# Gate strips and modulation tiles in another order, and two rings for streamed tiles, in a hybrid mLSTM, retention and SSD layer

## The chip, the cores and the metric

The kernel runs on one core of a Trainium2 chip. The metric is the device time of one execution in microseconds, lower is better. The engines are named as the profile names them: PE multiplies matrices (PEld is its weight load), DVE, ACT and POOL work on vectors, SP issues the transfers between memory and the chip.

## What is computed

One layer of a trunk for 384 tokens of width 2048 (128 context tokens and 256 latent tokens, which share all weights). What matters of the reference:

```python
mod = silu(c) @ w_mod + b_mod
sh_a, sc_a, g_a, sh_f, sc_f, g_f = split(mod, 6)
h = rmsnorm(x, norm_mix_g) * (1 + sc_a) + sh_a
q, k, v, ..., gl = split(h @ w_in)
gates = sigmoid(gl)
merged = gates[0] * (y_m @ w_br_m) + gates[1] * (y_r @ w_br_r) + gates[2] * (y_s @ w_br_s)
x = x + g_a * (merged @ w_out)
h = rmsnorm(x, norm_mlp_g) * (1 + sc_f) + sh_f
x = x + g_f * (square(relu(h @ w_ff1)) @ w_ff2)
```

`y_m`, `y_r` and `y_s` are the outputs of three branches (mLSTM, retention, SSD), whose chunked scans also return final states. All is in float32.

## The kernel before

**Products.** Every large product is cut into strips, and a strip into units (`strip`, line 114). A unit streams 512 KB of weights: four blocks of 128 rows by 256 columns (kind A, 24 matmuls with 384 columns) or two blocks by 512 columns (kind B5, 18 matmuls with 512 columns). Each operand is split into a rounded high part and a rest, and three products are added. So for each unit ACT rounds the raw tile into `whi` (line 88, called in line 155), DVE subtracts it to get `wlo` (line 91, called in line 156), and then PE multiplies. There are 568 such units behind a start section of 32 units. Raw tiles have a ring of 6 buffers (`RAWB`, line 54), `whi` and `wlo` one of 3 (`SPB`).

**Order.** The order of the work is written out by the Python program: `run_units` (line 213) goes through the list of units. For each it emits the loads that the ring has room for (`emit_raws`, line 135, all on SP's queue), the split of the unit two ahead (`emit_splits`, line 143), the matmuls, one step of the generators in the background (`bg_steps`: the scans of the branches), up to `pops` entries of the modulation's queue (`pop_mods`, line 391), and the eviction of the strip that ended before. Each engine runs its instructions in the order in which they were emitted. `later(n, f)` emits f n units on.

**Modulation.** Four of the six modulation vectors are computed beside the products, in 16 quarters of 512 columns, and each quarter in 8 tiles of 512 KB of `w_mod`: 128 tiles. `strip` puts a tile behind a unit whenever a counter reaches 1 (lines 122 to 125); the counter grows by the stage's `rate` at each unit, and falls by 1 for a tile, by 3 for the last tile of a quarter. Before the change a tile takes its place in the ring of raw tiles, in the order of the list. `mod_tile` (line 334) then puts the tile's work into the queue: with `mx=2` four multiply-adds on DVE (line 339); with `mx=0` two of them on DVE, two scalings on ACT (line 348) and two additions on POOL. The raw buffer counts as free when that work has been emitted (`raw_done`, line 129), in the order of the ring. A quarter ends with matmuls that add its sums over the partitions (`mod_end`, line 356), behind two empty entries of the queue.

**Stages.** After the start section: mLSTM (strips for q, k, v of four heads and for the output gate, 64 units), the strips for the convolution (SX, 24 units), four gate strips of branch 0 and the strips for z (16 units each), retention in two halves of 24 units (RQ, RK, RV, line 1371) with three gate strips of branch 0 between them, retention's gate (RG, line 1380, 16 units), the merge (line 1455 on), `w_out` (32 units), and the two products of the MLP (4 times 32 units of `w_ff1` and 32 of `w_ff2`).

**Gates.** Gates of branch 1 are computed in the start section, and seven strips of branch 0 ahead by `gate_ahead` (line 1168): the sigmoid goes to DRAM (`scr_g`), and the merge loads it back (`g_load`, line 1391). The merge goes through `seq` (line 1389): branch 1, branch 0, branch 2, eight strips each of two units; a gate strip of four units stands ahead of a strip whose gate isn't there yet: one of branch 0, and all eight of branch 2, whose gate is also multiplied by `Rs` on POOL (line 1403). `b_evac` (line 1407) multiplies by the gate on DVE and adds to `mg` on POOL.

**End of the merge.** After the last gate strip `mh_begin` (line 1432) gives the room of the layer's input to `mhi` and `mlo` and splits 14 of the 16 blocks of `mg` (`mg_split`, line 1440: ACT rounds, DVE subtracts); `merged_end` splits the last two, and the `w_out` strips begin.

**Retention's scans.** `r_scan` (line 1238) is a generator with 12 steps for a pair of heads. The two pairs of the second half are put into the background when RV's second strip is evicted. The eviction of RG's strip p waits, by emitting steps with nothing between them, until pair p is done (`r_evac_g`, line 1351).

Of the kernel before, what the change touches and what calls it, by code (L numbers as in the profile page):

```python
# [11 lines left out]
ALU = mybir.AluOpType  # L12
# [3 lines left out]
D = 2048  # L16
# [30 lines left out]
def hybrid_step(ctx: ExitStack, tc: tile.TileContext, cpack, x_prompt, x_sample, c, state_mlstm_C,  # L47
# [6 lines left out]
    RAWB, SPB = 6, 3  # L54
# [52 lines left out]
    raw_list, unit_list = [], []  # L107
    raws, splits, done = {}, {}, set()
# [5 lines left out]
    def strip(w, c0, kt, operand, evac, kind="A", row0=0, post=None, pre=None, sync=False, hold=0):  # L114
# [3 lines left out]
        for k0 in range(0, kt, uk):  # L118
# [4 lines left out]
            if mods and tune["due"] >= 1:  # L123
                m = mods.popleft() + (tune["mx"],)
                tune["due"] -= 3 if m[2] == 7 else 1
                raw_list.append((mod_src(*m[:3]), 2))
                unit_list.append((Block("M", m, None, KT), len(raw_list) - 1, 0, 1))
# [14 lines left out]

    def emit_splits(n):
        while pos["split"] < min(n, len(unit_list)):
            i = pos["split"]
            blk, ri, k0, uk = unit_list[i]
            emit_raws()
            while ri not in raws:
                pop_mods(1)
                emit_raws()  # L150
            if blk.kind != "M":
# [61 lines left out]
    def run_units():  # L213
        for i, (blk, ri, k0, uk) in enumerate(unit_list):
# [7 lines left out]
            if blk.kind == "M":  # L222
                mod_tile(*blk.operand, raws.pop(ri), ri)
                continue
# [109 lines left out]
    def mod_tile(m, q, r, mx, t, ri):  # L334
        t = r3(t, 2)

        def first():
# [3 lines left out]
            if mx < 2:  # L341
                half.append(second)
            else:
                raw_done(ri)

        def second():
# [3 lines left out]
            raw_done(ri)  # L350

        dq.append(first)
        if r == 7:
            dq.extend((None, None, lambda: mod_end(m, q)))
# [569 lines left out]
    for h in range(4):  # L924
        tune.update(rate=0.65 if h else 0.0, pops=2)
# [234 lines left out]
    tune["rate"] = 0.0  # L1160
# [7 lines left out]
    def gate_ahead(b, j, pool_, tag):  # L1168
        def f(ps):
            for i in range(2):  # L1170
# [4 lines left out]
                act.activation(out=sg, in_=ps[i][:, 0:T], func=AF.Sigmoid)  # L1175
                later(1, lambda i=i, sg=sg: sp.dma_start(out=scr_g[b * KT + 2 * j + i], in_=sg))
# [3 lines left out]
    tune.update(rate=0.25, pops=2, mx=2)  # L1180
# [189 lines left out]
    tune.update(rate=0.35, pops=2, mx=2)  # L1370
    for p in range(2):
# [3 lines left out]
        if p == 0:  # L1375
            tune["rate"] = 0.65
            for j in (5, 6, 7):
                gate_ahead(0, j, "hl", None)
            tune["rate"] = 0.35
# [27 lines left out]
    def b_evac(n):  # L1407
        def f(ps):
            b, j = seq[n]
            mg, sg = P["mg"], GG.pop(n)  # L1410
            for i in range(2):
# [3 lines left out]
                else:  # L1415
                    tt(dve, sg[:, i], ps[i][:, 0:T], sg[:, i], ALU.mult)
                    tt(pool, mg[:, k], mg[:, k], sg[:, i], ALU.add)
            g_load(n + 2)
# [13 lines left out]
    def mh_begin():  # L1432
# [4 lines left out]
        for k in range(14):  # L1437
            mg_split(k)
# [16 lines left out]
    tune.update(rate=0.65, pops=2, mx=0)  # L1455
    after = {7: lambda: load_branch(y_m), 15: lambda: load_branch(P["y_s"]), 23: lambda: bg.append(merged_end())}
    for n, (b, j) in enumerate(seq):
        if (b, j) not in ahead:
            strip(W, GL + b * D + 256 * j, KT, h_op, g_evac(n), post=mh_begin if n == 23 else None)
# [3 lines left out]
    tune.update(rate=0.5, pops=2)  # L1463
# [187 lines left out]
    for fc in range(4):  # L1651
        for j in range(8):
            tune.update(rate=0.8 if j else 0.0, pops=2 if j else 0)
# [92 lines left out]
```

## Time and profile before

| | us |
|---|---|
| three runs, median (lowest to highest) | 2813.42 (2808.92 to 2814.22) |
| the profiled execution's own time | 2814.81 |
| its span, first to last instruction | 2813.0 |

The page of the profile gives each engine's busy time over the span. The prediction goes by stages: the table of stretches gives the same busy times for a part of the span, the clock that TensorE was granted there (1.00 is 2.4 GHz, and 0.5 the lower level of 1.2 GHz) and the rate of transfers. The waits of an engine in a stretch name the instruction that ended its idle time: "PE gb L100 <- DVE wlo L91" is a matmul of a strip that waited for the rest part of its weights. PE's matmuls overlap and their ends are modelled, so its idle time is a little smaller than what a stop costs.

### The profile page before, as it was taken

How to read it: one execution, taken by the hardware profiler on the slowest of the kernel's cores; microseconds unless marked ns; L12 is line 12 of the kernel's file. 1: busy time of each engine (PE TensorE's matmuls, PEld its weight loads, DVE VectorE, ACT ScalarE, POOL GpSimd, SP SyncE). 2: the span in 40 equal slices, each digit the busy share in tenths (PEclk: the TensorE clock that was granted, in tenths of full speed). 3: DMA queues.
4: the chain of work that ended last, by engine and by line, in shares of the span. 5: the costliest groups of instructions: out<-in, count | busy, mean ns of one | idle time of the engine just before them, and what ended most of it. 6: DMA issues, size and time to landing. Idle time of an engine off the chain costs nothing. (4 is left out here: it accounts for less than half of the span.)

```text
span 2813.0 us, 38264 instructions
## 1 busy us (share of the span) xinstructions
PE 2736.7 (97%) x15109; PEld 2513.9 (89%) x15109; DVE 1558.1 (55%) x1883; ACT 1155.7 (41%) x1708; POOL 757.4 (27%) x588
## 2 busy tenths in 40 slices
PE   8999999999999999999999998999999999999998
PEld 7899988898998988989999877988899899889987
DVE  3666566645765465567876756773343334334434
ACT  5333444546643343544444445442233233323333
POOL 4200233512241111235766442441100100010012
PEclk9999999999999999999999998999999999999999
DMA  9955555545755555466666643564443344344442
GB/s 316 307 191 171 144 173 153 167 143 157 214 149 155 155 181 163 144 191 208 193 200 189 230 158 120 184 201 140 127 128 128 128 128 127 127 128 127 127 144 103
DMA packets 377835, 465.54 MB, mean 165 GB/s; under 512 B 20980, under 2 KB 277128, under 8 KB 376504
## 3 DMA queue, kind: packets, MB, share of 16 engines
q1 hardware_dynamic: 377656, 463.10, 53.4%
q8 instruction: 118, 1.93, 0.3%
q14 instruction: 61, 0.50, 0.1%
HBM read 449.47 MB, written 13.57 MB: 165 GB/s over the span
## 5 line engine op out<-in xcount | busy, mean ns | idle before, releaser
L91 DVE TENSOR_TENSOR wlo<-raw,whi 128x1024 fp32r<-128x1024 f32 x599 | 817.5, 1370 | 954.0 <-ACT whi L88 944.5
L88 ACT ACTIVATE whi<-raw 128x1024 fp32r<-128x1024 f32 x600 | 632.3, 1058 | 1002.9 <-PE gb L100 465.0
L100 PE MATMUL gb<-hhi,whi 128*128 128x384 f32 x1600 | 552.0, 345 | 9.4 <-ACT whi L88 4.2
L100 PE MATMUL gb<-hhi,wlo 128*128 128x384 f32 x1600 | 540.9, 338 | 11.6 <-DVE wlo L91 11.5
L100 PE MATMUL gb<-hlo,whi 128*128 128x384 f32 x1600 | 538.1, 336 | 0.4 <-DVE hlo L91 0.4
L91 POOL TENSOR_TENSOR macc<-macc,raw 128x512 f32<-128x512 f32 x194 | 326.2, 1682 | 351.2 <-issue 245.7
L100 PE MATMUL gb<-h2i,wlo 128*128 128x384 f32 x1024 | 345.0, 337 | 5.1 <-DVE wlo L91 5.1
L100 PE MATMUL gb<-h2l,whi 128*128 128x384 f32 x1024 | 345.3, 337 | 3.7 <-DVE h2l L1553 3.7
L100 PE MATMUL gb<-h2i,whi 128*128 128x384 f32 x1024 | 344.9, 337 | 2.5 <-ACT h2i L1549 1.6
L339 DVE SCALAR_TENSOR_TENSOR macc<-raw,cs,macc 128x512 f32<-128x512 f32 x318 | 324.9, 1030 | 6.6 <-DMA macc<-in_b_mod_dram 0.7
L100 PEld LDWEIGHTS gb<-hhi,whi 128*128 128x128 f32 x1600 | 303.1, 189 | 25.1 <-issue 8.8
L100 PEld LDWEIGHTS gb<-hhi,wlo 128*128 128x128 f32 x1600 | 302.5, 189 | 17.5 <-DVE wlo L91 17.3
L100 PEld LDWEIGHTS gb<-hlo,whi 128*128 128x128 f32 x1600 | 303.0, 189 | 1.7 <-DVE hlo L91 0.7
L91 POOL TENSOR_TENSOR x<-x,t 128x512 f32<-128x512 f32 x45 | 71.7, 1623 | 801.7 <-DVE t L91 801.7
L100 PEld LDWEIGHTS gb<-h2i,wlo 128*128 128x128 f32 x1024 | 193.9, 189 | 7.0 <-DVE wlo L91 7.0
L100 PEld LDWEIGHTS gb<-h2l,whi 128*128 128x128 f32 x1024 | 193.7, 189 | 6.3 <-DVE h2l L1553 6.1
L100 PE MATMUL gb<-whi,ahi 128*128 128x512 f32 x512 | 199.3, 389 | 0.0
L100 PE MATMUL gb<-whi,alo 128*128 128x512 f32 x512 | 199.2, 389 | 0.0
L100 PE MATMUL gb<-wlo,ahi 128*128 128x512 f32 x512 | 199.2, 389 | 0.0
L100 PEld LDWEIGHTS gb<-h2i,whi 128*128 128x128 f32 x1024 | 193.9, 189 | 4.8 <-ACT h2i L1549 1.8
L348 ACT ACTIVATE raw<-raw,cs 128x512 f32<-128x512 f32 x194 | 134.0, 717 | 69.7 <-DVE macc L339 62.5
L100 PE MATMUL gb<-yhi,whi 128*128 128x384 f32 x384 | 129.2, 336 | 1.1 <-ACT yhi L88 1.1
(415 smaller groups left out, 3923.3 us busy)
## 6 DMA issues: line engine op xcount, KB each, us to landing
raw<-in_w_in_dram SPq DMA_DIRECT2D x264, 512.0 KB
raw<-in_w_ff_dram SPq DMA_DIRECT2D x256, 512.0 KB
raw<-in_w_mod_dram SPq DMA_DIRECT2D x128, 512.0 KB
mraw<-in_w_mod_dram SPq DMA_DIRECT2D x32, 1024.0 KB
raw<-in_w_out_dram SPq DMA_DIRECT2D x32, 512.0 KB
raw<-in_w_br_r_dram SPq DMA_DIRECT2D x16, 512.0 KB
raw<-in_w_br_m_dram SPq DMA_DIRECT2D x16, 512.0 KB
raw<-in_w_br_s_dram SPq DMA_DIRECT2D x16, 512.0 KB
```

Source lines behind the costliest of these rows:

```text
L88: act.activation(out=out, in_=in_, func=AF.Copy, **kw)
L91: eng.tensor_tensor(out=out, in0=a, in1=b, op=op)
L100: pe.matmul(out, l, r, start=start, stop=stop)
L339: dve.scalar_tensor_tensor(out=macc[:, v], in0=t[:, kk], scalar=cs[:, 2 * r + kk, v:v + 1], in1=macc[:, v], op0=ALU.mult, op1=ALU.add)
L348: act.activation(out=t[:, kk], in_=t[:, kk], func=AF.Copy, scale=cs[:, 2 * r + kk, 1:2])
```

## The change

- Raw weight tiles get a ring of 4, and modulation tiles a ring of 2 of their own (`mr`). A modulation tile's load is emitted when the tile before it is reached (`emit_mod`); if the tile two before it has not been emitted yet, entries of the queue are emitted until it has.
- `mod_end` stands behind three empty entries.
- The rates change: 0.65 to 0.55 in mLSTM, 0 to 0.35 (`mx=2`) for SX, 0.25 to 0.2 for gates and z, 0.35 (0.65 in the gate strips) to 0.55 in retention, 0.65 to 0.45 in the merge, 0.5 to 0.25 in `w_out`, 0.8 to 0.6 in the MLP.
- Seven of the eight gate strips of branch 2 move from the merge to between retention's second half and RG, through `gate_ahead`; its eviction multiplies them by `Rs` on POOL. They use the buffers "sg" of retention's pool.
- `mh_begin` comes at strip 16 of the merge instead of 23, and `mg_split` is emitted for two blocks after each strip of branch 2 instead of 14 times at once.

```diff
--- before.py
+++ after.py
@@ -51,7 +51,7 @@
                 final_norm_g, y_prompt, y_sample, new_C, new_n, new_m, new_ret, new_ssd):
     nc = tc.nc
     act, dve, pool, pe, sp = nc.scalar, nc.vector, nc.gpsimd, nc.tensor, nc.sync
-    RAWB, SPB = 6, 3
+    RAWB, MRB, SPB = 4, 2, 3
 
     class Pool:
         def __init__(self, name, side="left", space=None):
@@ -104,8 +104,8 @@
         pe.transpose(out, in_, ident[0:n, 0:n])
 
 
-    raw_list, unit_list = [], []
-    raws, splits, done = {}, {}, set()
+    raw_list, mod_list, unit_list = [], [], []
+    raws, mraws, splits, done, mdone = {}, {}, {}, set(), set()
     pos = {"raw": 0, "split": 0, "used": 0}
     pend_evac, bg, delayed = [], deque(), []
     tune = {"bg": 1, "rate": 0.0, "due": 0.0, "pops": 3, "mx": 0}
@@ -123,8 +123,8 @@
             if mods and tune["due"] >= 1:
                 m = mods.popleft() + (tune["mx"],)
                 tune["due"] -= 3 if m[2] == 7 else 1
-                raw_list.append((mod_src(*m[:3]), 2))
-                unit_list.append((Block("M", m, None, KT), len(raw_list) - 1, 0, 1))
+                mod_list.append(mod_src(*m[:3]))
+                unit_list.append((Block("M", m, None, KT), len(mod_list) - 1, 0, 1))
 
     def raw_done(i):
         done.add(i)
@@ -140,15 +140,19 @@
             raws[pos["raw"]] = t
             pos["raw"] += 1
 
+    def emit_mod(j):
+        if j < len(mod_list):
+            while j >= MRB and j - MRB not in mdone:
+                pop_mods(1)
+            mraws[j] = strm([128, 1024], "mr", bufs=MRB)
+            sp.dma_start(out=r3(mraws[j], 2), in_=mod_list[j])
+
     def emit_splits(n):
         while pos["split"] < min(n, len(unit_list)):
             i = pos["split"]
             blk, ri, k0, uk = unit_list[i]
-            emit_raws()
-            while ri not in raws:
-                pop_mods(1)
+            if blk.kind != "M":
                 emit_raws()
-            if blk.kind != "M":
                 s = raws.pop(ri)
                 hi = strm([128, 1024], "whi", bufs=SPB, dt=F32R)
                 lo = strm([128, 1024], "wlo", bufs=SPB, dt=F32R)
@@ -211,6 +215,7 @@
                     mm(o, al[:, q], wh, False, k == n)
 
     def run_units():
+        emit_mod(0)
         for i, (blk, ri, k0, uk) in enumerate(unit_list):
             if k0 == 0 and blk.sync:
                 flush_evac()
@@ -220,7 +225,8 @@
             if k0 == 0 and blk.pre:
                 blk.pre()
             if blk.kind == "M":
-                mod_tile(*blk.operand, raws.pop(ri), ri)
+                mod_tile(*blk.operand, mraws.pop(ri), ri)
+                emit_mod(ri + 1)
                 continue
             wh, wl = splits.pop(i)
             end = k0 + uk == blk.kt
@@ -341,17 +347,17 @@
             if mx < 2:
                 half.append(second)
             else:
-                raw_done(ri)
+                mdone.add(ri)
 
         def second():
             for kk in range(mx, 2):
                 act.activation(out=t[:, kk], in_=t[:, kk], func=AF.Copy, scale=cs[:, 2 * r + kk, 1:2])
                 tt(pool, macc[:, 1], macc[:, 1], t[:, kk], ALU.add)
-            raw_done(ri)
+            mdone.add(ri)
 
         dq.append(first)
         if r == 7:
-            dq.extend((None, None, lambda: mod_end(m, q)))
+            dq.extend((None, None, None, lambda: mod_end(m, q)))
 
     def mod_end(m, q):
         p = bank()
@@ -922,7 +928,7 @@
     W = w_in[0]
     bg.append(gates())
     for h in range(4):
-        tune.update(rate=0.65 if h else 0.0, pops=2)
+        tune.update(rate=0.55 if h else 0.0, pops=2)
         strip(W, MQ + 256 * h, KT, h_op, m_evac_q(h))
         strip(W, MK + 256 * h, KT, h_op, m_evac_k(h))
         if h % 2 == 0:
@@ -1157,7 +1163,7 @@
         r_begin()
         yield
 
-    tune["rate"] = 0.0
+    tune.update(rate=0.35, mx=2)
     strip(W, SX + 1024, KT, h_op, s_conv(4))
     strip(W, SX + 1280, KT, h_op, s_conv(5))
     for j in range(4):
@@ -1173,11 +1179,13 @@
                 else:
                     sg = P[pool_]([128, T], "ga_", tag="ylo%d" % (4 + (2 * j + i) % 4))
                 act.activation(out=sg, in_=ps[i][:, 0:T], func=AF.Sigmoid)
+                if b == 2:
+                    tt(pool, sg, sg, P["Rs"], ALU.mult)
                 later(1, lambda i=i, sg=sg: sp.dma_start(out=scr_g[b * KT + 2 * j + i], in_=sg))
         ahead.add((b, j))
         strip(W, GL + b * D + 256 * j, KT, h_op, f)
 
-    tune.update(rate=0.25, pops=2, mx=2)
+    tune.update(rate=0.2, pops=2, mx=2)
     for j in range(4):
         gate_ahead(0, j, "s", "ac")
     for j in range(4):
@@ -1367,16 +1375,16 @@
         g_load(0)
         g_load(1)
 
-    tune.update(rate=0.35, pops=2, mx=2)
+    tune.update(rate=0.55, pops=2, mx=2)
     for p in range(2):
         strip(W, RQ + 512 * p, KT, h_op, r_evac_qk(p, "q"), "B5")
         strip(W, RK + 512 * p, KT, h_op, r_evac_qk(p, "k"), "B5")
         strip(W, RV + 512 * p, KT, h_op, r_evac_v(p), "B5")
         if p == 0:
-            tune["rate"] = 0.65
             for j in (5, 6, 7):
                 gate_ahead(0, j, "hl", None)
-            tune["rate"] = 0.35
+    for j in range(1, 8):
+        gate_ahead(2, j, "r", "sg")
     for p in range(4):
         strip(W, RG + 256 * p, KT, h_op, r_evac_g(p), post=r_end if p == 3 else None)
 
@@ -1415,6 +1423,8 @@
                 else:
                     tt(dve, sg[:, i], ps[i][:, 0:T], sg[:, i], ALU.mult)
                     tt(pool, mg[:, k], mg[:, k], sg[:, i], ALU.add)
+                if b == 2 and j < 7:
+                    later(1, lambda k=k: mg_split(k))
             g_load(n + 2)
         return f
 
@@ -1434,8 +1444,6 @@
         P["mh"] = Pool("mh", "left")
         P["mhi"] = P["mh"]([128, KT, T], "mhi", dt=F32R)
         P["mlo"] = P["mh"]([128, KT, T], "mlo", dt=F32R)
-        for k in range(14):
-            mg_split(k)
 
     def mg_split(k):
         rnd(P["mhi"][:, k], P["mg"][:, k])
@@ -1452,15 +1460,15 @@
         x2_begin()
         yield
 
-    tune.update(rate=0.65, pops=2, mx=0)
+    tune.update(rate=0.45, pops=2, mx=0)
     after = {7: lambda: load_branch(y_m), 15: lambda: load_branch(P["y_s"]), 23: lambda: bg.append(merged_end())}
     for n, (b, j) in enumerate(seq):
         if (b, j) not in ahead:
-            strip(W, GL + b * D + 256 * j, KT, h_op, g_evac(n), post=mh_begin if n == 23 else None)
+            strip(W, GL + b * D + 256 * j, KT, h_op, g_evac(n), post=mh_begin if n == 16 else None)
         strip((w_br_m, w_br_r, w_br_s)[b][0], 256 * j, 8, y_op, b_evac(n), post=after.get(n))
 
 
-    tune.update(rate=0.5, pops=2)
+    tune.update(rate=0.25, pops=2)
     def x2_begin():
         P["x"] = Pool("px", "right")
         x2 = P["x2"] = P["x"]([128, 3, D], "x2")
@@ -1650,7 +1658,7 @@
 
     for fc in range(4):
         for j in range(8):
-            tune.update(rate=0.8 if j else 0.0, pops=2 if j else 0)
+            tune.update(rate=0.6 if j else 0.0, pops=2 if j else 0)
             strip(w_ff1[0], 2048 * fc + 256 * j, KT, h2_op, f1_evac(j), sync=fc == 0 and j == 0,
                   post=h2_end if fc == 3 and j == 7 else None)
         for n in range(4):
```

## Rows read from the trace of the kernel before

**Rows 1.** The page, part 1: the span, and PE's busy time with its share.

```profile
span 2813.0 us, 38264 instructions
PE 2736.7 (97%) x15109; PEld 2513.9 (89%) x15109; DVE 1558.1 (55%) x1883; ACT 1155.7 (41%) x1708; POOL 757.4 (27%) x588
```

**Rows 2.** Busy time by stretch: start:end, length, engines' us (count), PE clock, DMA, GB/s.

```profile
290.00:568.00 278.00, 264.73 (x1398) 244.79 (x1397) 173.28 (x269) 133.14 (x217) 108.81 (x77) 0.98 0.54 159
...
850.00:1120.00 270.00, 267.37 (x1334) 231.57 (x1333) 152.76 (x193) 99.93 (x145) 51.51 (x65) 1.00 0.55 164
1120.00:1222.00 102.00, 95.43 (x591) 93.42 (x590) 52.66 (x70) 52.19 (x96) 27.93 (x33) 0.98 0.44 131
1222.00:1568.00 346.00, 345.55 (x2020) 344.91 (x2019) 262.30 (x234) 158.07 (x207) 216.77 (x134) 1.00 0.65 201
1568.00:1715.00 147.00, 139.47 (x628) 113.00 (x627) 87.80 (x83) 67.22 (x109) 62.85 (x38) 1.00 0.58 198
...
1745.00:1880.00 135.00, 128.91 (x727) 124.19 (x726) 109.25 (x107) 68.91 (x101) 59.85 (x34) 1.00 0.61 185
1880.00:2740.00 860.00, 860.00 (x4334) 779.53 (x4333) 337.48 (x351) 270.02 (x320) 73.47 (x46) 1.00 0.42 132
```

**Rows 3.** PE's waits from 290 to 568 us (mLSTM): us in total, times, longest.

```profile
PE gb L100 <- DVE wlo L91: 8.8, 8, 1.8
PE gb L100 <- ACT whi L88: 4.3, 3, 2.1
```

**Rows 4.** SP's waits, whole span: weight loads behind POOL's modulation additions.

```profile
SPq L139 <- POOL macc L91: 302.1, 91, 8.9
```

**Rows 5.** ACT's waits, whole span: the largest on a weight load.

```profile
ACT whi L88 <- DMA raw<-in_w_out_dram: 12.1, 3, 5.8
```

**Rows 6.** PE's waits from 1180 to 1225 us (from RG to the merge).

```profile
PE sb L104 <- POOL o L91: 3.3, 1, 3.3
PE gb L100 <- ACT yhi L88: 1.1, 1, 1.1
PE sb L100 <- ACT kT L1281: 0.7, 1, 0.7
```

**Rows 7.** PE's waits from 1570 to 1595 us (first units of w_out).

```profile
PE gb L100 <- DVE wlo L91: 4.8, 3, 3.1
```

**Rows 8.** DVE in order of time, 1566 to 1577 us: start, us, instruction.

```profile
1565.52 9.46 DVE L91 TENSOR_TENSOR mlo<-mg,mhi 128x384 fp32r<-128x384 f32 x14 [0.94 <-ACT mhi L88]
1574.91 1.21 DVE L91 TENSOR_TENSOR wlo<-raw,whi 128x1024 fp32r<-128x1024 f32 x1
```

**Rows 9.** PE's waits from 1745 to 1880 us (first product of the MLP).

```profile
PE gb L100 <- DVE wlo L91: 5.1, 5, 1.2
```

**Rows 10.** PE's waits from 1595 to 1690 us (w_out).

```profile
PE gb L100 <- DVE wlo L91: 1.6, 2, 1.0
PE sb L100 <- POOL macc L91: 1.1, 1, 1.1
```

**Rows 11.** PE's waits from 860 to 1180 us (retention).

```profile
PE gb L100 <- DVE wlo L91: 1.0, 2, 0.8
```

**Rows 12.** DVE's groups from 850 to 1120 us (retention): busy us, mean ns.

```profile
L91 DVE TENSOR_TENSOR wlo<-raw,whi 128x1024 fp32r<-128x1024 f32 x59 | 72.9, 1248 | 81.6 <-ACT whi L88 76.8 <-PE sb L100 4.7
L339 DVE SCALAR_TENSOR_TENSOR macc<-raw,cs,macc 128x512 f32<-128x512 f32 x76 | 59.0, 797 | 1.3
L91 DVE TENSOR_TENSOR rt<-sb,cr 128x256 f32<-128x256 f32 x16 | 6.0, 420 | 8.0 <-POOL qtok L91 4.0 <-POOL ktok L91 4.0
```

**Rows 13.** DVE's and POOL's groups from 1222 to 1568 us (merge).

```profile
L91 DVE TENSOR_TENSOR wlo<-raw,whi 128x1024 fp32r<-128x1024 f32 x80 | 129.5, 1624 | 48.5 <-ACT whi L88 48.4
L339 DVE SCALAR_TENSOR_TENSOR macc<-raw,cs,macc 128x512 f32<-128x512 f32 x84 | 99.7, 1186 | 2.4 <-DMA macc<-in_b_mod_dram 0.7
...
L91 POOL TENSOR_TENSOR sg<-sg,Rs 128x384 f32<-128x384 f32 x15 | 21.2, 1435 | 3.3 <-ACT sg L1402 3.3
```

**Rows 14.** ACT in order of time, 1578 to 1585 us.

```profile
1583.69 0.53 ACT L88 ACTIVATE mhi<-mg 128x384 fp32r<-128x384 f32 x1 [4.41 <-POOL mg L91]
```

## The prediction

> **What bounds the kernel now.** The page comes first: PE is busy for 2736.7 of 2813.0 us [rows 1]. So the change, which leaves every product in place, can only win idle time of PE and time at the lower clock. The table of stretches tells where that is: PE idles 13.3 us in mLSTM (278 less 264.73), 2.6 in retention, 6.6 around RG, 0.5 in the merge, 7.5 in w_out, 6.1 in the first product of the MLP, and nothing in the 860 us from 1880 on, which have hardly any modulation tiles [rows 2]. The clock adds a little: 0.98 over 278 us costs 5.6 us, over the 102 us around RG 2.0.
>
> The waits say for what. In mLSTM 13.1 us are waits for `wlo` and `whi`, eleven stops of at most 2.1 us [rows 3]: no weights were missing, but ACT or DVE had other work ahead of the split. Around RG it is the scan of retention [rows 6], in w_out the split of `mg` [rows 7, 8] and tiles [rows 10], in the MLP tiles again [rows 9]. Loads are late less often: SP stood 302 us, 91 times, behind POOL's additions, because a raw buffer held a modulation tile [rows 4], yet the largest of five like groups in which ACT waited for a weight load is 12.1 us [rows 5].
>
> **The change part by part.** The sum is made against the profiled execution, 2814.81 us: the span and 1.8 us around it that stay. It stands 1.4 us above the median of the runs shown.
>
> Going through the counter of lines 122 to 125 with the old and the new rates gives where the 128 tiles fall, before and after: mLSTM 25 and 22, SX 0 and 6, the gates of branch 0 with z 7 and 5, retention with its three gate strips 19 and 27, the seven moved strips 0 and 12, RG 5 and 8, merge 44 and 19, w_out 10 and 5, first MLP product 18 and 14, the product behind it 0 and 10. Tiles with `mx=2` rise from 31 to 58: each swaps two scalings on ACT and two additions on POOL for two multiply-adds on DVE.
>
> 1. *End of retention.* The last two pairs of scans need 24 steps; between RV's end and the eviction of RG's last strip there are 16 units, one step each, so some eight steps run with nothing between them. That shows as PE waits of 3.3, 0.7 and, for what follows the late gate, 1.1 us, 5.1 of 6.6 us idle [rows 2, 6]; the clock fell in the same stretch. With the 28 units of the moved strips ahead of RG there are 44 units for 24 steps. I take 5 us and 1.5 of the clock's 2.0: **-6.5**, from -8 to -3 (the last split of `y_r` may still be late).
>
> 2. *Split of the merged blocks.* 14 subtractions run as one block of 9.46 us on DVE, with the next `wlo` behind them [rows 8]; PE waits 4.8 us at the first units of w_out [rows 7]. Two at a time behind each of seven strips, they lie beside 8 us of matmuls. **-4.5**, from -4.8 to -2.5 (the last two blocks stay at the end).
>
> 3. *mLSTM.* 13.3 us idle and 5.6 of clock over 25 tiles are 0.75 us for a tile. Three tiles fewer are 2.3; stops come where a tile meets scan work, so wider spacing helps more than in proportion. **-4**, from -9 (half of it) to +3 (the tiles fall on worse units).
>
> 4. *MLP.* 5.1 us of waits for `wlo` over 18 tiles [rows 9]. At a rate of 0.8 a unit has, on DVE, 0.8 x 2 multiply-adds of 1.19 us and a `wlo` of 1.62 (as in the merge, whose tiles are of the same kind [rows 13]), and evictions: close to a unit's 4.2 us (4,334 matmuls of rows 2 at 21 a unit, the mean of 24 and 18, are 206 units in 860 us). At 0.6 it is 0.5 us less, so runs of eight tiles no longer pile up; but ten tiles now fall into the second product. **-4**, from -6 to +3 (ten more at the same 0.3 us).
>
> 5. *w_out.* Ten tiles, 2.7 us [rows 10]; half of them. **-1**, from -2.7 to 0.
>
> 6. *SX.* Six tiles where none were. By retention's row, 1.0 us of waits over its tiles [rows 11], they cost 0.2 us; by mLSTM's 0.75 each, 4.5. They are of retention's kind (`mx=2`). **+1.5**, nearer to the first, as scans run here too.
>
> 7. *Tiles in retention.* 47 tiles where 24 were, over 104 units instead of 76. Each is four multiply-adds of 0.80 us on DVE [rows 12], 3.2 us at once. DVE was busy 57% here [rows 2]; 23 more tiles add 73 us, and 28 more units 35 of `wlo`, over 115 us more of PE. That makes some 65% to 70%, below the merge's 76%, where PE lost 0.5 us in 346 [rows 2]. Bounds by the row of retention, +1, and by mLSTM's 0.75 for each of 47 tiles, +34. I take **+3**: the work is bursty, but POOL is idle for 81% of the time.
>
> 8. *New waits.* `mg_split` on ACT now waits for POOL's addition with the next `whi` behind it; one such wait of 4.4 us is in the trace [rows 14] and cost PE under 0.2 us of rows 7, because splits run two units ahead. Seven of them: 0 to 1.4 us. The stores of the moved gates hold buffers that the scans' squares need, on DVE, ahead of `wlo`: four places, bounded by 0 and 1 us each. Fourteen stores and seven loads of 384 KB, and `mh_begin` at strip 16, are hidden under a rate of transfers that falls with the tiles. **+0.5**, from 0 to +5.
>
> 9. *The rings.* Weights now run four raw tiles ahead whatever POOL does, some 17 us at 4.2 us a unit. A full ring of six had 25, but only where no tile sat in it. What it can win is the part of ACT's waits [rows 5] that reached PE; against it, the modulation load waits on SP for the buffer of the tile two before, with weights behind it in the queue, up to 8.9 us [rows 4], which 17 us cover. A tile's load has two to four units ahead of its use. **-1**, from -3 to +2. The third empty entry of `mod_end` is nothing: one unit later, 16 times, beside other work.
>
> 10. *Gates and z.* Two tiles fewer: **-0.5**, from -1.5 to 0. The 25 tiles that leave the merge win nothing, as PE idles 0.5 us there.
>
> Sum: -6.5 - 4.5 - 4 - 4 - 1 + 1.5 + 3 + 0.5 - 1 - 0.5 = -16.5, so 2798.3 for an execution like the profiled one, and 1.4 less, **2797 us**, as a median.
>
> **A rule of the Trainium skill against one part.** In retention, with POOL busy 19% of the time, a `wlo` takes 1.25 us and a multiply-add 0.80; in the merge, with POOL at 63%, 1.62 and 1.19 [rows 2, 12, 13]. The Trainium skill (SBUF — State Buffer, section "SBUF: two separate sides") says that a DVE instruction with two SBUF inputs and a GpSimd (POOL) instruction that reads SBUF exclude each other for the whole instruction. By that rule the 14 multiplications by `Rs`, now on POOL amid retention's DVE work, each hold a DVE instruction for up to their own 1.44 us [rows 13], 20 us of DVE; were none of it hidden, the sum would be +3.5 and the time 2817. The rows speak for hidden: fifteen of them stood in the merge beside 0.5 us of idle PE [rows 2, 13].
>
> **The rivals.**
> *More is won.* If the stops of mLSTM come mostly from weights and splits that arrive late because tiles sit in their ring, all 18.9 us of term 3 could go instead of 4: 2782. For it: SP's 302 us [rows 4]. Against it: rows 3 name `wlo` and `whi`, and only a small part of ACT's waits are for loads [rows 5]. Chance 0.12.
> *The gain is given back.* Tiles cost the same wherever they stand: terms 3 to 5 vanish (+9), retention's 23 more tiles cost half of mLSTM's price (+8 instead of +3): 2797 + 9 + 5 = 2811. For it: the number of tiles is the same. Against it: the price of a tile in the rows goes from 0.04 to 0.75. Chance 0.14.
> *Slower.* DVE becomes the bound in bursts in retention. An eviction of RQ or RK has eight multiplications of 0.42 us (two groups of 16 like the one shown, over four evictions) [rows 12]: 3.4 us, two tiles 6.4, two `wlo` 2.5, together 12.3 us against the two units, 8.4 us, by which splits run ahead. If that happens at most evictions and in the scans too, a tile there costs what it costs in mLSTM, 0.75 us, 47 times: +34 instead of +3, 2828. It decides once retention's tiles cost over 0.4 us each. Against it: at the old rate it is 0.04. Chance 0.12.
> That the rings don't do what they say, because both kinds of load stay in one queue of SP, changes term 9 by 1 to 3 us and stays within the forecast.
>
> **How the numbers follow.** The forecast has 0.62, with a range of its own of 2786 to 2807 (terms 3, 4 and 7 some 10 us either way). The whole range, 2783 to 2815, reaches to the rival of a larger gain and takes in the gain given back; it leaves out the slower one and half of the larger gain. About 0.2% (5.6 us) is what a measurement can tell from no change: faster than 2807.8 is 0.73 (0.61 and 0.12), the same 0.15 (0.14 and 0.01), slower 0.12.
>
> **What would show it.** After: no wait of PE for `o` near RG's end and no low clock there; no block of 14 `mlo`; SP's waits on POOL's additions well below 302 us; PE idle in mLSTM about 10 us, in the MLP about 3, in retention under 8 over its longer stretch. The forecast is wrong if retention idles over 20 us, or if ACT or DVE wait long for loads of `mr`.

## The result, and the profile after

The changed kernel takes 2836.39 us (median of four runs, 2833.29 to 2839.46) beside 2812.18 (2808.92 to 2814.22) of the kernel before on the same chip: a ratio of 1.0083 [1.0070, 1.0095]. The forecast was 2797 us in a range of 2783 to 2815, so both the sign and the range were wrong.

PE's own line of the page shows 92.5 us in which it is not busy (2836.0 less 2743.5), where it was 76.3 before [rows 1]:

```profile
span 2836.0 us, 38143 instructions
PE 2743.5 (97%) x15109; PEld 2520.8 (89%) x15109; DVE 1521.5 (54%) x1937; ACT 1122.5 (40%) x1656; POOL 635.7 (22%) x534
```

The table of stretches answers to [rows 2], with the same columns. In order: start, mLSTM, retention, the moved gate strips, RG, merge, `w_out`, the first product of the MLP with its opening (norm and transposes), and this product behind its opening. The last line is the kernel before, for the same work as the line above it.

```profile
0.00:224.00 224.00, 200.59 (x1618) 177.78 (x1619) 118.23 (x217) 89.83 (x151) 48.58 (x48) 0.98 0.83 259
299.00:568.00 269.00, 260.02 (x1401) 243.00 (x1401) 165.30 (x263) 129.56 (x211) 98.42 (x71) 0.99 0.55 161
858.00:1143.00 285.00, 273.30 (x1341) 234.92 (x1340) 172.19 (x224) 98.42 (x143) 48.68 (x65) 0.98 0.54 166
1143.00:1293.00 150.00, 139.66 (x831) 136.49 (x830) 82.70 (x104) 62.58 (x105) 30.58 (x37) 0.98 0.54 163
1293.00:1362.00 69.00, 69.00 (x406) 69.00 (x405) 45.74 (x52) 24.46 (x31) 11.15 (x9) 1.00 0.63 200
1362.00:1602.00 240.00, 239.42 (x1398) 239.10 (x1397) 159.32 (x177) 99.81 (x131) 106.26 (x73) 1.00 0.62 200
1602.00:1736.00 134.00, 134.00 (x610) 110.09 (x609) 59.91 (x59) 55.75 (x90) 34.98 (x24) 1.00 0.54 187
1736.00:1893.00 157.00, 146.40 (x789) 140.18 (x789) 112.03 (x135) 83.00 (x138) 55.99 (x38) 0.93 0.50 154
1760.00:1893.00 133.00, 129.84 (x730) 127.41 (x731) 92.84 (x109) 68.94 (x103) 43.66 (x27) 0.99 0.56 170
...
1740.00:1880.00 140.00, 133.91 (x749) 129.19 (x749) 113.27 (x115) 72.60 (x109) 59.85 (x34) 0.99 0.59 179
```

What was aimed at was won: mLSTM idles 9.0 us where it was 13.3, RG and `w_out` not at all where they idled 6.6 and 7.5, and the first product of the MLP 3.2 behind its opening where it was 6.1. (The line from 1736 on, with 10.6 us and a clock of 0.93, has the opening in it, which [rows 2] leaves out: from 1738 to 1760 PE idles 7.5 of 22 us at a clock of 0.62, and in the kernel before, from 1717 to 1740, 7.6 of 23 at 0.68.) But retention idles 11.7 instead of 2.6 and the moved strips 10.3, and the start is 9 us longer. The waits of the whole span say what is late (the first two lines are SP's queue, the others PE, DVE and ACT):

```profile
SPq L139 <- DVE wlo L91: 1897.5, 524, 16.7
SPq L148 <- POOL macc L91: 80.9, 26, 7.5
...
PE gb L100 <- DVE wlo L91: 37.3, 30, 3.7
DVE macc L345 <- DMA macc<-in_b_mod_dram: 13.5, 5, 3.4
DVE W L837 <- DMA Tb<-scr: 11.2, 4, 3.2
PE gemv L100 <- DMA mraw<-in_w_mod_dram: 11.2, 7, 3.1
DVE macc L345 <- DMA mr<-in_w_mod_dram: 10.8, 8, 1.9
PE gb L100 <- ACT whi L88: 10.3, 7, 3.4
DVE jk L91 <- DMA scr_g<-ga__10169: 5.0, 1, 5.0
...
ACT whi L88 <- DMA raw<-in_w_in_dram: 3.3, 1, 3.3
```

Weights are no longer late: ACT's waits for weight loads are 3.3 us in all, where one of five groups alone had 12.1 [rows 5]. Late now are the transfers that stand between them on SP's queue: DVE waits 63 us for rows of `b_mod`, modulation tiles, the scans' inputs and stores of gates (the lines shown, the three other `jk` of 5.0, 4.9 and 4.9, `Cb` 4.5 and a state 3.1), where before it waited 9 us for transfers, of which `Cb` with 3.8 was the largest group. The timeline shows how one of them becomes late (start, duration, queue or engine; SP, then POOL, DVE and PE):

```profile
1937.38 0.38 SPq L139 DMA_DIRECT2D raw<-in_w_ff_dram  x1
1937.87 0.56 SPq L333 DMA_DIRECT2D macc<-in_b_mod_dram  x2
...
1932.82 0.95 POOL L338 MEMSET macc<- 128x1024 f32 x1 [14.89 <-DMA scr_mod<-macc]
...
1935.67 1.69 DVE L91 TENSOR_TENSOR wlo<-raw,whi 128x1024 fp32r<-128x1024 f32 x1
1940.75 4.00 DVE L345 SCALAR_TENSOR_TENSOR macc<-mr,cs,macc 128x512 f32<-128x512 f32 x4 [3.39 <-DMA macc<-in_b_mod_dram]
1944.67 4.51 DVE L91 TENSOR_TENSOR wlo<-raw,whi 128x1024 fp32r<-128x1024 f32 x2
...
1947.01 0.50 PE L100 MATMUL gb<-wlo,ahi 128*128 128x512 f32 x1 [2.46 <-DVE wlo L91]
```

POOL has cleared `macc` at 1933.77, and the row of `b_mod` could go there at once. But the weight load ahead of it on SP's queue goes into the buffer that DVE's subtraction frees, which ends at 1937.36. Only then do both transfers start. The row lands at 1940.7, DVE has stood 3.39 us for it, four multiply-adds follow, then two `wlo` that are late, and PE stops for 2.46 us.

This is not one case alone. From the end of POOL's clearing to the start of the row's transfer there are 0.0 us before (median of the 16 quarters) and 3.8 after. Of the 14 stores of moved gates, 12 start 2.1 to 2.6 us after POOL has finished the gate. The first of them stands behind a weight load that starts when a `wlo` ends, at 1175.23:

```profile
1172.16 1.02 POOL L91 TENSOR_TENSOR ga__10169<-ga__10169,Rs 128x384 f32<-128x384 f32 x1 [12.62 <-ACT ga__10169 L1181]
...
1173.44 1.79 DVE L91 TENSOR_TENSOR wlo<-raw,whi 128x1024 fp32r<-128x1024 f32 x1 [3.78 <-ACT whi L88]
...
1175.26 0.39 SPq L139 DMA_DIRECT2D raw<-in_w_in_dram  x1
1175.75 0.45 SPq L1184 DMA_DIRECT2D scr_g<-ga__10169  x1
```

From the first `whi` of a stage to the first of the next, the time went as follows (us against the kernel before, each from the one profiled execution; the last two columns are experiments told below):

| stage (term of the prediction) | forecast | after | one ring | three edits |
|---|---|---|---|---|
| start (none) | 0 | +9.1 | 0.0 | -1.6 |
| mLSTM (3) | -4 | -9.9 | -11.3 | -15.1 |
| SX (6) | +1.5 | +2.1 | +2.0 | +2.0 |
| gates of branch 0 and z (10) | -0.5 | +9.1 | +8.8 | +4.0 |
| retention with its gate strips (7) | +3 | +15.8 | +14.3 | +13.2 |
| moved strips, RG, merge (1) | -6.5 | -2.0 | -14.5 | -14.4 |
| `w_out` (2 and 5) | -5.5 | -3.6 | -3.7 | -3.7 |
| first two products of the MLP (4) | -4 | +2.4 | -8.4 | -5.7 |
| rest | 0 | 0.0 | 0.0 | 0.0 |
| sum (with terms 8 and 9, -0.5) | -16.5 | +23.0 | -12.8 | -21.3 |

In the MLP it is the second product that lost: 139.9 us from first `whi` to first `whi` instead of 130.0, the first one took 155.4 instead of 163.0 (by PE's own first matmuls 6.9 more and 4.5 less). The stop of the timeline stands in the second. Over the last 808.5 us, which have hardly any tiles, none of these kernels differs.

### The profile page after: what moved, and what is told of

Its sections match the earlier page's. It is cut to its first block, busy times and chain, and to the rows that moved or that the text cites. A ratio compares the mean times of both kernels' runs of the same rounds, so it can differ in the third digit from the quotient of the medians.

```text
span 2836.0 us, 38143 instructions
## 1 busy us (share of the span) xinstructions
PE 2743.5 (97%) x15109; PEld 2520.8 (89%) x15109; DVE 1521.5 (54%) x1937; ACT 1122.5 (40%) x1656; POOL 635.7 (22%) x534
## 5 line engine op out<-in xcount | busy, mean ns | idle before, releaser
L91 DVE TENSOR_TENSOR wlo<-raw,whi 128x1024 fp32r<-128x1024 f32 x599 | 792.8, 1329 | 947.2 <-ACT whi L88 945.5
L345 DVE SCALAR_TENSOR_TENSOR macc<-mr,cs,macc 128x512 f32<-128x512 f32 x372 | 314.0, 858 | 34.3 <-DMA macc<-in_b_mod_dram 13.5
L91 POOL TENSOR_TENSOR macc<-macc,mr 128x512 f32<-128x512 f32 x140 | 222.1, 1586 | 334.8 <-issue 164.6
L100 PE MATMUL gb<-ylo,whi 128*128 128x384 f32 x384 | 128.4, 334 | 0.6 <-DVE ylo L91 0.6
```

Source lines behind the costliest of these rows:

```text
L91: eng.tensor_tensor(out=out, in0=a, in1=b, op=op)
L100: pe.matmul(out, l, r, start=start, stop=stop)
L345: dve.scalar_tensor_tensor(out=macc[:, v], in0=t[:, kk], scalar=cs[:, 2 * r + kk, v:v + 1], in1=macc[:, v], op0=ALU.mult, op1=ALU.add)
```

## The experiments

**First set: one suspect each, on the changed kernel.** The theory was that SP's queue is in step with DVE; the rivals were the ring of the start section, the buffer of the squares, and the tiles' rates.

*e1_start_ring.* The start section streams its weights with as many buffers as `RAWB` says; the change cut that from six to four. Here it uses the two `mr` tiles too.

```diff
-        while todo and held[todo[0][0]] < (4 if todo[0][0] == "m" else RAWB):
+        while todo and held[todo[0][0]] < (4 if todo[0][0] == "m" else RAWB + MRB):
...
-            t = start([128, 2048], "mraw", bufs=4) if kind == "m" else raw_tile()
+            if kind == "m":
+                t = start([128, 2048], "mraw", bufs=4)
+            else:
+                t = raw_tile() if nw[0] % 6 < 4 else strm([128, 1024], "mr", bufs=MRB)
+                nw[0] += 1
```

> The changed kernel, but the start section keeps six weight tiles in flight (four of the ring and the two modulation buffers, which nothing else uses there). Theory A (the start section shares RAWB, so its ring fell from 6 to 4 and the loads stop more often): the main loop's first split comes back from 224 us to about 215, PE's waits for the start section's modulation loads fall from 11 us to about 2, and the time is about 2827. Rival (these loads are merely late by chance, memory being the limit there): no change, 2836.

2828.33 us, ratio 1.0054 [1.0039, 1.0069]: 8.1 us less than the changed kernel. The first `whi` behind the start comes at 214.8 us, as before, where it was 223.9, and PE's wait for `mraw` is 3.1 us (11.2 without the edit). So the start section is some 9 us of the loss. (With four buffers, the first `whi` came at 223.9 to 228.3 us in the profiled executions of e2 to e4 and of the changed kernel, with six at 213.1 to 214.9.)

*e2_squares_buf.* The squares of retention's scans get another buffer than the stores of the moved gates.

```diff
-            jk = Pr([128, T], "jk", tag="sg", bufs=2)
+            jk = Pr([128, T], "jk", tag="PT")
```

> The changed kernel, but the squares of retention's scan use the buffer of PT instead of the ring 'sg' that the moved gate strips store from. Theory B (DVE waits four times 5 us for the stores of the gates, with the next wlo behind it): these four waits vanish, the strips at 1137 to 1287 us lose some 8 us of stops and a spell of the lower clock, time about 2826. Rival (the longer stops there come from tiles of four multiply-adds on DVE): the stops stay, under 3 us are won, 2834.

2826.59, ratio 1.0050 [1.0035, 1.0065]: 9.8 us less. All four waits of `jk` are gone, and the moved strips take 139.3 us instead of 150.0.

*e3_load_later.* A weight load is emitted one split later. It still goes into the buffer that the same `wlo` frees, but that `wlo` was emitted a unit before, and what is emitted in between now stands ahead of the load on SP; weights run three tiles ahead instead of four.

```diff
-        while pos["raw"] < min(len(raw_list), pos["used"] + RAWB):
+        while pos["raw"] < min(len(raw_list), pos["used"] + RAWB - 1):
```

> The changed kernel, but a weight load is emitted one split later, so that it asks for a buffer that was read one unit before (three loads ahead instead of four). Theory C (with its own ring every weight load waits on SP for the wlo that was only just emitted, 1898 us in all, and every small transfer behind it is late): SP's waits for wlo fall by more than half, DVE's waits for b_mod, modulation tiles, scan inputs and gate stores (over 50 us) mostly go, and the time falls to about 2820. Rival (weights need the depth): ACT waits for weight loads, and the time is 2840 or more.

2805.49 (ten runs, 2803.18 to 2809.07), ratio 0.9976 [0.9967, 0.9985]: 30.9 us less, and faster than the kernel before. Its waits:

```profile
SPq L139 <- DVE wlo L91: 1589.4, 477, 14.6
...
PE gb L100 <- DVE wlo L91: 25.0, 23, 3.2
...
DVE macc L345 <- DMA mr<-in_w_mod_dram: 4.4, 3, 2.3
DVE macc L345 <- DMA macc<-in_b_mod_dram: 4.1, 2, 3.4
DVE W L837 <- DMA Tb<-scr: 2.2, 3, 1.4
```

DVE's waits for transfers fell from 63 to 13 us, those for `jk` to nothing, without e2's edit, and PE's for `wlo` from 37.3 to 25.0, while ACT still waits only 3.4 us for weights. A row of `b_mod` now starts 2.2 us after the clearing (median, 3.8 in the changed kernel), and all 14 stores of moved gates as soon as POOL is done, ahead of the weight load:

```profile
1163.43 1.02 POOL L91 TENSOR_TENSOR ga__10167<-ga__10167,Rs 128x384 f32<-128x384 f32 x1 [12.62 <-ACT ga__10167 L1181]
...
1164.48 0.34 SPq L1184 DMA_DIRECT2D scr_g<-ga__10167  x1
...
1166.54 0.38 SPq L139 DMA_DIRECT2D raw<-in_w_in_dram  x1
```

The moved strips take 137.4 us, a little less than with e2's edit, so the 30.9 us take in e2's 9.8, and the gains of the first three edits must not be added. One number came out otherwise than expected: SP's waits for `wlo` went down by a sixth, not by half. SP is far ahead of the other engines and always waits for something, so the sum of its waits says little; which instruction it waits for, and what stands behind it, decides.

*e4_old_rates.* The changed kernel with the rates of before.

```diff
-        tune.update(rate=0.55 if h else 0.0, pops=2)
+        tune.update(rate=0.65 if h else 0.0, pops=2)
...
-    tune.update(rate=0.55, pops=2, mx=2)
+    tune.update(rate=0.35, pops=2, mx=2)
...
-    tune.update(rate=0.45, pops=2, mx=0)
+    tune.update(rate=0.65, pops=2, mx=0)
...
-            tune.update(rate=0.6 if j else 0.0, pops=2 if j else 0)
+            tune.update(rate=0.8 if j else 0.0, pops=2 if j else 0)
```

> The changed kernel with the rates of before (and no tiles in SX); rings and order as changed. Theory D (the loss in retention and SX is the 29 more tiles there, four multiply-adds on DVE each): SX, gates and retention come back by 20 us or more, mLSTM loses its 10 us again, time about 2822 or below. Rival (rings and buffers, theories A to C): retention keeps most of its loss, and with mLSTM's gain gone the time is 2836 or above.

2883.53, ratio 1.0251 [1.0234, 1.0268]: 47.1 us more than the changed kernel. Retention's second half becomes shorter (109.9 us instead of 122.4), but PE's waits for the two halves of the weights come to 79.9 us:

```profile
PE gb L100 <- DVE wlo L91: 44.0, 43, 3.1
PE gb L100 <- ACT whi L88: 35.9, 14, 5.5
```

So the new rates are, in sum, no cause of the loss; with these rings they save 47 us. In retention alone they are: with the old rates its halves and three gate strips take 271.4 us, as before the change, and 287.3 with the new ones. There the first theory was right (SX, gates with z, and retention give 18.3 us back, where 20 or more were expected) and the rival, by which retention keeps most of its loss, wrong; by the total it is the other way round.

**Second set: the rings alone, the order alone, and all edits.**

*e5_rings_only.* The kernel before, with the rings of 4 and 2 and `emit_mod` (the start section as in e1), and nothing else of the change.

```diff
-    RAWB, SPB = 6, 3
+    RAWB, MRB, SPB = 4, 2, 3
...
             if blk.kind == "M":
-                mod_tile(*blk.operand, raws.pop(ri), ri)
+                mod_tile(*blk.operand, mraws.pop(ri), ri)
+                emit_mod(ri + 1)
```

> The kernel before with the two rings alone (start section kept at six weight tiles; order and rates of before). If the rings are what costs (each load on SP waits for the newest wlo, with all other transfers behind it), the time is far above before: the changed kernel with the old rates took 2884 us, of which 9 are the start section, so about 2865. If the old rates cost so much only together with the moved strips, the time is near before, 2813 to 2825.

2857.72, ratio 1.0155 [1.0140, 1.0170]. The rings alone cost 43 us at the old rates (2814.34 for the kernel before on the same chip):

```profile
SPq L139 <- DVE wlo L91: 1880.5, 525, 14.0
...
PE gb L100 <- ACT whi L88: 29.7, 8, 8.4
DVE macc L345 <- DMA macc<-in_b_mod_dram: 29.6, 6, 10.5
DVE macc L345 <- DMA mr<-in_w_mod_dram: 28.5, 13, 8.3
```

*e6_shared_ring.* The other half: the new order, rates and empty entries, with one ring of six as before.

```diff
-    RAWB, MRB, SPB = 4, 2, 3
+    RAWB, SPB = 6, 3
...
-                mod_tile(*blk.operand, mraws.pop(ri), ri)
-                emit_mod(ri + 1)
+                mod_tile(*blk.operand, raws.pop(ri), ri)
```

> The changed kernel with the one ring of six of before; order of strips, splits of the merged blocks, rates and empty entries as changed. If the rings are the step that failed, this is near what the prediction gave for the rest, about 2800 (start section as before, the waits of the scans' squares at most in part). If order and rates cost as well, it stays above before, 2820 or more.

2802.15, ratio 0.9958 [0.9943, 0.9973]. The forecast's sum without the rings was -15.5 us; this is -12.8 in the profiled execution (2800.2 us of span). So the rest of the prediction held in its sum, and the rings are what turned it. That the sum held is in part luck: by the table, stages that came out worse than forecast (22.9 us, gates with z and retention above all) and better (19.7, mLSTM, the merge with its strips, the MLP) nearly cancel.

*e7_three.* The changed kernel with the edits of e1, e2 and e3, the last two again:

```diff
-            jk = Pr([128, T], "jk", tag="sg", bufs=2)
+            jk = Pr([128, T], "jk", tag="PT")
...
-        while pos["raw"] < min(len(raw_list), pos["used"] + RAWB):
+        while pos["raw"] < min(len(raw_list), pos["used"] + RAWB - 1):
```

> The changed kernel with the three edits of the first runs together: start section with six weight tiles, squares in the buffer of PT, weight loads one split later. If the start section's loss is separate from the other two, 2805 less 8 to 10: about 2796. Squares: at most 2 us more, as the later loads already freed the stores. If the start's loss is absorbed later, 2805.

2793.27 (2792.53 to 2795.85), ratio 0.9930 [0.9915, 0.9944]. It beats both kernels, by 43.1 us the changed one, and e6 by 9. So with later loads, two rings are worth more than one in this order (e6 lacks e2's edit, but its moved strips take 137.5 us as here). Its page:

```profile
span 2791.7 us, 38183 instructions
PE 2726.9 (98%) x15109; PEld 2510.5 (90%) x15109; DVE 1526.1 (55%) x1937; ACT 1122.2 (40%) x1656; POOL 634.4 (23%) x534
```

*e8_three_rates.* e7 with retention's two halves at the old 0.35, the three gate strips between them at 0.35 as well (0.65 before), and the merge at the old 0.65.

```diff
-    tune.update(rate=0.55, pops=2, mx=2)
+    tune.update(rate=0.35, pops=2, mx=2)
...
+    tune["rate"] = 0.55
...
-    tune.update(rate=0.45, pops=2, mx=0)
+    tune.update(rate=0.65, pops=2, mx=0)
```

> The same, and the tiles of retention's two halves go back to a rate of 0.35 (0.55 stays in the moved strips and RG), the merge to 0.65 in exchange. With the old rates the two halves took 18 us less than in the changed kernel. If that is the price of the tiles there, about 10 us under the kernel with the three edits, 2786; if the tiles cost the same in the merge, no difference.

2795.88, ratio 0.9939 [0.9923, 0.9956]. Retention's halves go from 106.2 and 119.8 us to 101.9 and 111.2, 12.9 less: what is left of retention's loss in e7 is the tiles (PE's waits for split weights there fall from 10.2 to 2.7 us). But the tiles that go back to the merge cost there what they no longer cost here (239.3 to 250.2 us), and `w_out` loses 2.8. In all nothing is won.

**Third set: is the step the whole of the rings' cost?**

*e9_before_later.* The kernel before with e3's edit (its ring has six buffers).

```diff
-        while pos["raw"] < min(len(raw_list), pos["used"] + RAWB):
+        while pos["raw"] < min(len(raw_list), pos["used"] + RAWB - 1):
```

> The kernel before, one shared ring of six, with a load emitted one split later (five ahead). If waiting for the newest wlo costs by itself, before gains a little too, 2 to 6 us, 2809, as some of its loads also stood in step. If its loads were out of step already because tiles sat in the ring, no change, 2813; if it needs the depth, slower.

2814.02, ratio 1.0007 [0.9997, 1.0016]: no difference in the time. By stages of the profiled execution, gates and z take 6.0 us less, and mLSTM, the merge and `w_out` together 6.6 more: in the kernel before the edit has nothing to take back in sum.

*e10_rings_later.* e5 with the same edit.

```diff
-        while pos["raw"] < min(len(raw_list), pos["used"] + RAWB):
+        while pos["raw"] < min(len(raw_list), pos["used"] + RAWB - 1):
```

> The kernel before with the two rings alone (2858 us), and weight loads one split later. If the step in which a load waits is the cause, the 45 us go: 2815 or less. If it is the tile ring of two, whose loads come too late at a rate of 0.8, most stays: 2840 or more. In between, both have a share, in proportion.

2819.05, ratio 1.0020 [1.0011, 1.0029]: the rings cost 5 us where they cost 43, so moving every load by one split takes back 38. A row of `b_mod` starts 2.6 us after the clearing (median), in e5 6.0.

```profile
DVE macc L345 <- DMA mr<-in_w_mod_dram: 9.7, 8, 4.7
DVE macc L345 <- DMA macc<-in_b_mod_dram: 7.9, 3, 5.5
```

*e11_three_and_three.* e1 with rings of three and three.

```diff
-    RAWB, MRB, SPB = 4, 2, 3
+    RAWB, MRB, SPB = 3, 3, 3
```

> The changed kernel with six tiles in flight in the start section (2828 us), and rings of three weight tiles and three modulation tiles instead of four and two; a load is emitted in step with the newest split, as in the changed kernel. If the step is the cause, it stays at 2828 or more, though no more loads run ahead than in the kernel with later loads. If the tiles' short ring is, or if fewer loads ahead help by themselves, about 2805.

2819.83, ratio 1.0024 [1.0012, 1.0036]: 8.5 us less than e1, between the two outcomes that were expected. SP is still in step (1962.1 us of waits for `wlo`). DVE no longer waits for rows of `b_mod`, and 5.9 us for `mr` (8.8 in e1), but as long as before for the four `jk`. Two things changed, and the run does not part them: weights run three ahead, and SP waits 14.3 us for POOL's additions to free a tile's buffer, where it was 79.9 in e1. Together they are worth less than a load emitted one split later, which has three weights ahead too.

*e12_two_later.* e7 with loads two splits later.

```diff
-        while pos["raw"] < min(len(raw_list), pos["used"] + RAWB - 1):
+        while pos["raw"] < min(len(raw_list), pos["used"] + RAWB - 2):
```

> The kernel with the three edits (2793 us), but loads two splits later, two ahead. If any wait of SP for a fresh wlo still costs, a little less, 2790. If two units of some 4 us are too few for a load, which took up to 5 us here, ACT waits for loads, and the time is 2800 or more.

2795.49, ratio 0.9938 [0.9923, 0.9952]: no gain over e7, and not the 2800 of the second outcome either. Now weights are late, ACT waits 46 us for them:

```profile
ACT whi L88 <- DMA raw<-in_w_ff_dram: 21.2, 6, 5.4
ACT whi L88 <- DMA raw<-in_w_in_dram: 18.2, 7, 5.1
```

One later is the best of the three distances, or as good as two.

## Why the prediction was wrong

**Term 9, the rings, is the step that failed: -1 us in the prediction, +43 alone; e3, which only moves the loads in the queue, takes 31 us off the changed kernel.** Those 31 contain e2's 9.8 and come on top of the start section's 9. The term asked whether weights come late, and there it was right: SP's waits on POOL's additions fell from 302.1 us [rows 4] to 80.9, and the weights in hand covered what was left. It did not ask who waits behind a weight load. "A tile's load has two to four units ahead of its use" counts from the place at which the load is written, but it starts when SP comes to it, and SP stands at the weight load before it until the newest `wlo` is done. A ring that holds weights alone and is kept full puts nearly every weight load there (524 of 568 waited for a `wlo`). The prediction named the modulation loads with weights queued behind them and not the weight loads with the modulation, its `b_mod` rows, the scans' transposed rows and the gates' stores behind them. Both of its own tests did show: DVE waits 10.8 us for `mr` and 13.5 for the rows of `b_mod`, and retention with the moved strips idles 22.0 us. That the place of the load is the cause, and not the smaller number of weight buffers, is shown by e3 and e10, which have fewer weights ahead still and win 31 and 38 us; fewer loads ahead, in step as before, won 8.5 us at most (e11, unless its third tile buffer did harm). The ring of six was spared in fact: SP already stood at the row of `b_mod` when POOL cleared its place (0.0 us in the median, before, in e9 and in e6). Why is argued only: a tile in the ring that had not been worked off held back the loads behind it, so that SP waited for POOL's additions 91 times [rows 4] and for DVE's multiply-adds 33 times, and its loads fell out of step. E9 fits this, since there one split later changes nothing in sum.

**The start section was left out: 0 in the prediction, +9.1 us.** The prediction read `RAWB` as the ring of the 568 units; line 431 uses the same name for the 32 units before them. E1 gives it back.

**Term 8 had the place and not the size.** The stores of the moved gates were seen to hold buffers that the squares need, "four places, bounded by 0 and 1 us each"; they were 5.0, 5.0, 4.9 and 4.9, and e2 won 9.8 us. The bound left out SP: 12 of the 14 stores stood behind a weight load for 2.1 to 2.6 us, and with e3's edit neither that nor the waits of `jk` are left. With one ring they are 4.9, 2.6 and 1.0.

**Term 7 was too small: +3 in the prediction, +13.2 with all three edits.** Part of it is the bursts of the slower rival, at less than half of its price: PE's waits for split weights in retention are 11.6 us after, where they were 1.0 [rows 11], and 10.2 with the three edits. The other half lies in PE's busy time, 274.7 us of 285 with the edits and 268.4 of 271 before; some 3 us of that is the clock, 0.99 and 1.00, and the rest was not followed. The prediction took the mean share of DVE (57%, to some 65% to 70%), which does not show that a tile's four multiply-adds, an eviction and two `wlo` come together:

```profile
PE gb L100 <- DVE wlo L91: 10.9, 6, 3.7
PE gb L100 <- ACT whi L88: 0.7, 1, 0.7
```

These are PE's waits in retention, from 858 to 1143 us: six stops of up to 3.7, while DVE is busy for 60% of the stretch. E4 and e8 showed that with the lower rate retention's loss goes (0.0 and 0.8 us are left), and e8 that the tiles cost as much elsewhere: the rival of the gain given back was right for these tiles, for the merge's free tiles (0.5 us of idle time in 346 [rows 2]) were not there to be had once its gate strips had gone.

**Terms 1 to 5 were right in kind, and their gain in sum larger than taken.** With the three edits mLSTM wins 15.1 us (-4 in the prediction, from -9), near the 18.9 of the rival of a larger gain; but 11.3 of it come with one ring too, so most of it is not the ring that this rival named. The moved strips, RG and the merge win 14.4 (-6.5), of which RG alone is 10.9, 80.0 to 69.1 us; no wait for `o` is left, and RG's clock is 1.00. `w_out` wins 3.7 (-5.5): the block of 14 is gone, and no stop there. The MLP wins 5.7 (-4), in the first product (163.0 to 152.5 us), with 4.8 given back in the second as its new tiles come. Term 6 measured +2.0 (+1.5). Term 10 had the wrong sign: +4.0 instead of -0.5, and against e9, which has the later loads but the old order, +9.9. One stop there is the 3.5 us that PE waits for the convolution's scan (`xd` on POOL, 2.5 before); the rest was not followed further. The sum of the errors partly cancels: -21.3 us with the three edits, -16.5 in the prediction.

**The rule on locked ports** (the Trainium skill, SBUF — State Buffer, section "SBUF: two separate sides") agrees with this trace in its direction for `wlo`, and cost nothing that shows here. Retention has no such multiplications in it, and the groups on DVE are as before [rows 12]:

```profile
L345 DVE SCALAR_TENSOR_TENSOR macc<-mr,cs,macc 128x512 f32<-128x512 f32 x105 | 79.3, 777 | 10.8 <-DMA macc<-in_b_mod_dram 5.0 <-DMA mr<-in_w_mod_dram 2.3 <-DMA s<-in_state_ret_dram 1.4
L91 DVE TENSOR_TENSOR wlo<-raw,whi 128x1024 fp32r<-128x1024 f32 x60 | 73.4, 1237 | 62.8 <-ACT whi L88 62.8
```

In the moved strips, with the 14 multiplications by `Rs` and the scans' other work on POOL beside them, a `wlo` takes 1337 ns instead of 1237: 0.1 us for each of 29, 3 us of DVE in place of the 20 that stood as the bound. The multiply-adds, which read two such inputs as well, show nothing of it (767 ns instead of 777). That the multiplications cause the 3 us is not shown. With the three edits PE idles 1.2 of 137 us there, so they were hidden.

Not tried: small transfers on the queue of another engine. They would then not stand behind a weight load's wait; what that is worth is open.

## What to carry to other kernels

A prefetch that shares an in-order queue with small transfers should not wait for the newest consumer: emit it one step later, so that what is emitted in the meantime stands ahead of it in the queue, even at the price of one buffer of prefetch. When a ring is split or resized, look for every use of its size and for what stands behind each load in the queue, and not only for whether the load itself is in time. A share of busy time does not price a burst: count what falls on one engine between two deadlines. And compare stretches that hold the same work: the opening of a stage, in one window and not in the other, looks like a loss.

## What was not expected

Better supply of weights went with a slower kernel: ACT's waits for weight loads fell from some 40 us (the five groups of which [rows 5] shows the largest) to 3.3, and the time rose by 24 us. And a distance that matters by 31 us in one kernel (e3) and by 38 in another (e10) is worth nothing in the kernel before (e9, 1.0007 [0.9997, 1.0016]): one ring of six and two rings of the same total size differ by 43 us, nearly all of it in the place that a load has in the queue.
